# Two sums of w_down's blocks, moved from VectorE in the projection stage to GpSimd in the up stage

## Chip, core and metric

One core of a Trainium2 chip runs the whole kernel. The metric is the device time of one execution in microseconds (us), a median over runs. Engines are named as in the profile: PE is TensorE (PEld its weight loads), DVE is VectorE, ACT is ScalarE, POOL is GpSimd, and SP is the engine that only issues DMAs here, all of them, from one queue and in program order.

## What is computed

A decoder block on 1024 tokens of width 1024: two attention branches mixed by sigmoid gates, then a gated MLP with a causal convolution. The change concerns the end of the mixer and the MLP:

```python
y = jax.nn.sigmoid(g_mla) * (o_mla @ w_o_mla) + jax.nn.sigmoid(g_fox) * (o_fox @ w_o_fox)
...
u = h @ w_up                                   # 1024 x 5632
u = conv_b + sum(conv_w[j] * up[:, j:j + s] for j in range(CONV_WIDTH))
gate, val = u[..., :D_FF], u[..., D_FF:]       # D_FF = 2816
return (jax.nn.silu(gate) * val) @ w_down      # w_down: 2816 x 1024
```

All matrices are float32.

## The kernel before

Each float32 operand is split in a rounded high part (`hi_act`, by ACT, line 82) and the rest (`lo_dve`, line 91, by DVE, or `lo_pool`, line 94, by POOL), and each product is three matmuls, at lines 101 to 103. The MLP's two products run as 2x2 block products with seven instead of eight multiplications, which need sums of blocks of the operands as well. For w_down two such sums are needed, N1 and T2. w_down's rows lie in 22 blocks of 128; for each pair of them (m = 0 to 10), N1 is the left half (columns 0 to 511) of the even block minus its right half, and T2 is the right half of the odd block plus N1. They are made ahead of time, written to DRAM scratch (`dram_N`, `dram_T` in the profile), and read back in the last stage.

**Projection stage** (`mix_and_up`, trace 764 to 862 us). A loop over eight feature blocks d: two products from `w_o_mla` and `w_o_fox` (48 matmuls of 512 columns in all), times the sigmoid gates loaded to tiles `raw` (four buffers in a ring), added, and split into `y`. Two "late rows" are computed in this loop, for g = 5 with d = 1 and for g = 2 with d = 3 (`late_row`): a 512 KB tile is loaded from scratch `dram_acc` into a `raw` buffer, split by ACT and DVE, and summed over partitions by PE (line 311). In the same loop `sum_right` makes N1 and T2 for 11 blocks m of w_down: it loads `dx` (512 KB) and `dz` (256 KB), two buffers each, DVE subtracts (line 973) and adds (line 974), and two stores of 256 KB go out.

**Up stage** (`ffn_up`, trace about 1000 to 1416 us). A loop over 22 columns j of w_up. `operands(j + 1)` loads the next column's two 512 KB tiles `wr` (two buffers) and makes its block sums on DVE (lines 1213 to 1217) and the splits `sh`, `sl`, `vh`, `vl`. PE runs the products of column j; the first four columns have their first and last product for the left half done earlier and have 60 matmuls, later ones 84. DVE reads the banks (lines 1293, 1295), then the convolution (line 1246), a product (line 1306) and, in odd columns, four sums (`stored`, lines 1327 to 1330; on DVE up to j = 7, on POOL later). A second product onto a bank can only start when DVE has read the first one (line 1293, then the product with N4).

**Order.** A scheduler orders the instructions of each engine ahead of time, by its own estimates, with the data dependences kept; so an instruction can stand far from where the code writes it. SP waits at each DMA for what it needs (the data to store, a free buffer, which is the completion of the store that last read it), and all later DMAs wait behind it.

Of the kernel before, what the change touches and what calls it, by code (L numbers as in the profile page):

```python
# [8 lines left out]
F32 = mybir.dt.float32  # L9
# [4 lines left out]
ALU = mybir.AluOpType  # L14
# [58 lines left out]
class Block:  # L73
# [887 lines left out]
    def load_right(self, pool, m):  # L961

        x, z = pool([P, D], F32, "dx", 2), pool([P, 512], F32, "dz", 2)
        self.dma(x, self.a["w_down"][0, 2 * m * P : (2 * m + 1) * P, :])
        self.dma(z, self.a["w_down"][0, (2 * m + 1) * P : (2 * m + 2) * P, 512:1024])
        return m, x, z

    def sum_right(self, pool, d):

        G, V = self.nc.gpsimd.tensor_tensor, self.nc.vector.tensor_tensor  # L970
        lower, upper = HALVES
        for m, x, z in self.blocks:
            V(out=x[:, lower], in0=x[:, lower], in1=x[:, upper], op=ALU.subtract)
            V(out=z, in0=z, in1=x[:, lower], op=ALU.add)
            self.dma(self.place("N1", m), x[:, lower])
            self.dma(self.place("T2", m), z)
        self.blocks = [self.load_right(pool, self.unsummed.pop(0)) for _ in range(2 if 0 < d < 5 else d < 7)]


    def mix_and_up(self):  # L980
# [5 lines left out]
        op, oh, ol = self.op, self.oh, self.ol  # L986
        self.blocks, self.unsummed = [], list(range(NJ // 2))
        for d in range(KD):
# [23 lines left out]
            if d == 4:  # L1012
                self.conv_weights()
            self.sum_right(op, d)
            for late, g in ((1, 5), (3, 2)):
# [232 lines left out]
    def ffn_up(self, tp):  # L1248
# [13 lines left out]
        def first_product(j):  # L1262
            if j < EARLY:
                x = up([P, 512], F32, "p1", 2)
                self.dma(x, self.d_early[j][:, 0, :])
                return x

        def gate(j):
            return (None, None, None) if j < EARLY else self.gate_operands(j)

        ahead, p1 = self.operands(0, gate(0)), first_product(0)
        for j in range(NJ):
            a11, a12, a22, s1, s2, s3, s4 = ahead
# [10 lines left out]
            self.product(x6, s2, "T2", False)  # L1284
            t = copied(x6)
            ug, uv = up([P, S], F32, "u", 6), up([P, S], F32, "u", 6)
            if j < EARLY:
# [19 lines left out]
            if j < NJ - 1:  # L1307
                self.stored(j, act)
        self.last_act = act

# [235 lines left out]
```

## Time and profile before

| | us |
|---|---|
| median of 3 runs (1632.31 to 1634.5) | 1633.96 |
| the profiled execution, its own time | 1631.67 |
| its span, first to last instruction | 1629.9 |
| projection stage, matmuls of d = 0 to 7 | about 764 to 862 |
| residual, second norm and first products of the MLP | about 862 to 1000 |
| up stage | about 1000 to 1416 |
| down stage | about 1416 to 1630 |

A profile's number for an engine is its busy time; PE is the busiest, and its idle time in a stage is time that the stage lost, if nothing else is behind. A row of the timeline gives start, duration, engine, line and tiles, and in brackets how long the engine sat idle before it and what ended that. The granted clock (PEclk) is the share of TensorE's full clock; 0.5 is 1.2 GHz, 1.0 is 2.4 GHz.

### The profile page before, as it was taken

What the parts mean: (1) busy time and instruction counts of PE and PEld (TensorE: products, weight loads), DVE (VectorE), ACT (ScalarE), POOL (GpSimd) and SP (SyncE); (2) the same over time, 40 slices, a digit from 0 to 9 for tenths busy, and PEclk for the clock granted to TensorE, in tenths of its full rate; (3) what the DMA queues carried; (4) which work ended last, traced back from release to release, by engine and by line L of the source; (5) the groups of instructions that cost most, each with busy time, mean ns of one, the idle gap of its engine ahead of it and who ended that gap; (6) DMA issues with size and microseconds to landing.
All of it is one profiled execution on the core that took longest, in us unless ns stands there. A gap on an engine that the chain in (4) does not pass through costs nothing.

```text
span 1629.9 us, 21135 instructions
## 1 busy us (share of the span) xinstructions
PE 1552.7 (95%) x7574; PEld 1274.8 (78%) x7574; DVE 1086.5 (67%) x1741; ACT 776.4 (48%) x1337; POOL 356.8 (22%) x317
## 2 busy tenths in 40 slices
PE   7899989999997999999899978999999999999997
PEld 3778868888886888887687867778888888788886
DVE  5755666566655566575655786988777677746578
ACT  3434345445443555565333444555555455435345
POOL 1322024676671312302020111000011111101010
PEclk9999999999998999999999999999999999999999
DMA  8435487766455434435885425343333332587852
GB/s 286 147 106 162 165 251 198 211 190 184 149 163 134 122 91 128 116 86 203 295 298 194 143 90 168 117 123 97 112 104 111 114 108 99 189 327 288 293 186 104
DMA packets 195191, 271.11 MB, mean 166 GB/s; under 512 B 13090, under 2 KB 114146, under 8 KB 193742
## 3 DMA queue, kind: packets, MB, share of 16 engines
q1 hardware_dynamic: 195086, 269.77, 52.4%
q8 instruction: 59, 0.97, 0.2%
q14 instruction: 46, 0.38, 0.1%
HBM read 187.14 MB, written 70.00 MB: 158 GB/s over the span
## 4 chain that ended last, share of the span: by engine, by line
PE 43%; DVE 4%; DMA 4%; ACT 2%; issue 1%; SPq 0%; ACTq 0%; DVEq 0%
PE ps_mm L101 5%; PE ps_mm L103 5%; PE ps_mm L102 5%; PE ps_sd L101 4%; PE ps_sd L103 4%; PE ps_sd L102 4%; PE ps_x L102 2%; PE ps_x L103 2%; PE ps_x L101 2%; PE ps_y L102 2%; PE ps_y L101 2%; PE ps_y L103 2%; DMA wr_wr<-in_w_up_dram 1%; DVE up_u L1246 1%; DMA o_raw<-dram_acc 1%
## 5 line engine op out<-in xcount | busy, mean ns | idle before, releaser
L101 PE MATMUL psA_fill<-hT_hi,ws_wh 128*128 128x512 f32 x352 | 150.0, 426 | 0.0
L758 ACT ACTIVATE att_p<-psA_s,small_soft 128x128 f32<-128x128 f32 (+7 forms) x128 | 94.8, 740 | 105.4 <-DVE small_soft L752 103.8
L103 PE MATMUL psA_fill<-hT_hi,ws_wl 128*128 128x512 f32 x352 | 139.3, 396 | 0.0
L102 PE MATMUL psA_fill<-hT_lo,ws_wh 128*128 128x512 f32 x352 | 139.3, 396 | 0.0
L94 POOL TENSOR_TENSOR ws_wl<-wr_wr,ws_wh 128x512 fp32r<-128x512 f32 x62 | 83.2, 1346 | 244.6 <-ACT ws_wh L82 221.7
L752 DVE TENSOR_REDUCE small_soft<-psA_s 128x1 f32<-128x128 f32 (+7 forms) x128 | 96.0, 751 | 52.9 <-PE psA_s L750 52.2
L748 PE MATMUL psA_s<-opn_k,opn_q 96*128 96x256 f32 (+7 forms) x480 | 114.6, 359 | 17.3 <-DMA opn_k<-opn_stg 10.9
L1246 DVE SCALAR_TENSOR_TENSOR up_u<-up_u,cw_cw,up_u 128x1023 f32<-128x1023 f32 x88 | 110.7, 1277 | 4.2 <-ACT up_u L1244 4.1
L748 PEld LDWEIGHTS psA_s<-opn_k,opn_q 96*128 96x128 f32 (+1 forms) x480 | 82.1, 192 | 26.7 <-issue 16.6
L760 DVE TENSOR_SCALAR att_p<-att_p,small_soft 128x128 f32<-128x128 f32 (+7 forms) x128 | 86.1, 672 | 4.1
L91 DVE TENSOR_TENSOR att_ptl<-psA_pt,att_pth 128x512 fp32r<-128x512 f32 x96 | 66.0, 687 | 33.3 <-ACT att_pth L82 33.0
L777 PE MATMUL psA_pt<-const_ident,att_p 128*128 128x128 f32 x576 | 86.3, 272 | 0.0
L82 ACT ACTIVATE ring_ah<-ring_ar 128x1024 fp32r<-128x1024 f32 (+1 forms) x41 | 40.4, 985 | 87.5 <-PE ps_x L102 56.9
L91 DVE TENSOR_TENSOR ring_al<-ring_ar,ring_ah 128x1024 fp32r<-128x1024 f32 (+1 forms) x41 | 49.9, 1216 | 45.9 <-ACT ring_ah L82 45.9
L103 PEld LDWEIGHTS psA_fill<-hT_hi,ws_wl 128*128 128x128 f32 x352 | 66.4, 189 | 15.7
L82 ACT ACTIVATE uw_sh<-uw_s 128x1024 fp32r<-128x1024 f32 x44 | 46.7, 1062 | 61.8 <-PE ps_mm L102 29.2
L289 POOL TENSOR_TENSOR att_acc<-att_acc,att_lw 128x512 f32<-128x512 f32 x56 | 74.9, 1337 | 4.2
L101 PEld LDWEIGHTS psA_fill<-hT_hi,ws_wh 128*128 128x128 f32 x352 | 67.4, 191 | 9.6
L102 PEld LDWEIGHTS psA_fill<-hT_lo,ws_wh 128*128 128x128 f32 x352 | 66.9, 190 | 9.7
L91 DVE TENSOR_TENSOR uw_gl<-wr_wr,uw_gh 128x1024 fp32r<-128x1024 f32 x24 | 29.5, 1232 | 65.9 <-ACT uw_gh L82 64.4
L1328 POOL TENSOR_TENSOR up_u<-up_u 128x512 f32<-128x512 f32 x7 | 9.0, 1288 | 263.9 <-DVE up_u L1306 263.9
L82 ACT ACTIVATE att_pth<-psA_pt 128x512 fp32r<-128x512 f32 x96 | 57.2, 595 | 19.8 <-PE psA_pt L777 16.2
(444 smaller groups left out, 4555.6 us busy)
## 6 DMA issues: line engine op xcount, KB each, us to landing
wr_wr<-in_w_up_dram SPq DMA_DIRECT2D x48, 512.0 KB
att_lw<-in_w_ada_dram SPq DMA_DIRECT2D x64, 256.0 KB
wr_wr<-in_w_in_dram SPq DMA_DIRECT2D x28, 512.0 KB
ring_br<-in_w_down_dram SPq DMA_DIRECT2D x24, 512.0 KB
dram_S<-up_u SPq DMA_DIRECT2D x44, 256.0 KB
ring_ar<-dram_S SPq DMA_DIRECT2D x20, 512.0 KB
dram_A<-up_u SPq DMA_DIRECT2D x33, 256.0 KB
ada_wada<-in_w_ada_dram SPq DMA_DIRECT2D x16, 512.0 KB
```

The source lines that it names most:

```text
L82: self.nc.scalar.activation(out, in_, AF.Copy, scale=scale)
L91: self.nc.vector.tensor_tensor(out=out, in0=in_, in1=f32(hi), op=ALU.subtract)
L94: self.nc.gpsimd.tensor_tensor(out=out, in0=in_, in1=f32(hi), op=ALU.subtract)
L101: mm(ps, lhsT=lh, rhs=rh, start=start, stop=False, skip_group_check=onto)
L102: mm(ps, lhsT=lh, rhs=rl, start=False, stop=False, skip_group_check=onto)
L103: mm(ps, lhsT=ll, rhs=rh, start=False, stop=stop, skip_group_check=onto)
L748: mm(o, lhsT=l, rhs=r[:, keys], start=n_ == 0, stop=diag is None and n_ == len(passes) - 1)
L752: nc.vector.tensor_reduce(out=st[:, 0:1], in_=view(s), axis=AX.X if i < 4 else AX.XY, op=ALU.max, negate=True)
L758: nc.scalar.activation(po, view(s), AF.Exp, bias=st[:, 0:1], accum_out=st[:, 1:2])
L760: nc.vector.tensor_scalar(out=pr, in0=pr, scalar1=st[:, 2:3], scalar2=None, op0=ALU.mult)
L777: nc.tensor.transpose(pt[:, n * 256 + e * P : n * 256 + (e + 1) * P], pr[:, kb * P : (kb + 1) * P], self.ident)
L1246: nc.vector.scalar_tensor_tensor(out=dst[:, back:], in0=u[:, : S - back], scalar=cw[:, tap, jj : jj + 1], in1=dst[:, back:], op0=ALU.mult, ...
```

## The change

The sums go from the projection stage to the up stage, from DVE to POOL, and from two buffers of each tile to one:

```diff
     def load_right(self, pool, m):
-        x, z = pool([P, D], F32, "dx", 2), pool([P, 512], F32, "dz", 2)
+        x, z = pool([P, D], F32, "dx"), pool([P, 512], F32, "dz")
         ...
-    def sum_right(self, pool, d):
-        G, V = self.nc.gpsimd.tensor_tensor, self.nc.vector.tensor_tensor
+    def sum_right(self, m, x, z):
+        G = self.nc.gpsimd.tensor_tensor
         lower, upper = HALVES
-        for m, x, z in self.blocks:
-            V(out=x[:, lower], in0=x[:, lower], in1=x[:, upper], op=ALU.subtract)
-            V(out=z, in0=z, in1=x[:, lower], op=ALU.add)
-            self.dma(self.place("N1", m), x[:, lower])
-            self.dma(self.place("T2", m), z)
-        self.blocks = [self.load_right(pool, self.unsummed.pop(0)) for _ in range(2 if 0 < d < 5 else d < 7)]
+        G(out=x[:, lower], in0=x[:, lower], in1=x[:, upper], op=ALU.subtract)
+        G(out=z, in0=z, in1=x[:, lower], op=ALU.add)
+        self.dma(self.place("N1", m), x[:, lower])
+        self.dma(self.place("T2", m), z)
 ...
     def mix_and_up(self):
-        self.blocks, self.unsummed = [], list(range(NJ // 2))
-            self.sum_right(op, d)
 ...
     def ffn_up(self, tp):
-                x = up([P, 512], F32, "p1", 2)
+                x = up([P, 512], F32, "p1", 1)
         ahead, p1 = self.operands(0, gate(0)), first_product(0)
+        block = self.load_right(up, 0)
         for j in range(NJ):
             ...                                  # products N1 and T2 of column j
+            if j % 2 and j < NJ - 1:
+                block = self.load_right(up, (j + 1) // 2)
             ...                                  # the rest of column j
+            if j % 2 == 0:
+                self.sum_right(*block)
```

`p1` holds a finished first product of an early column; it loses a buffer as well.

In the order that results, three places matter. The first is SP's queue in the projection stage, ahead of the load of the second late row (`dram_acc2`). Before (`o_dx`, `o_dz` are the tiles of w_down, `dram_N12` and the like the scratch for the sums):

```order
L79 DMA dram_N12_103_186<-o_dx_26_8087 128x512
L79 DMA dram_T22_109_192<-o_dz_27_8088 128x512
L79 DMA dram_N14_104_187<-o_dx_28_8091 128x512
L79 DMA dram_T24_110_193<-o_dz_29_8092 128x512
L79 DMA o_dx_32_8182<-in_w_down_dram 128x1024
L79 DMA o_dz_33_8183<-in_w_down_dram 128x512
L79 DMA o_dx_34_8186<-in_w_down_dram 128x1024
L79 DMA o_dz_35_8187<-in_w_down_dram 128x512
L79 DMA o_raw_36_8190<-dram_acc2_43_126 128x1024
```

After, at the same load:

```order
L79 DMA o_raw_20_8074<-dram_gate3_20_103 128x1024
L79 DMA o_raw_21_8077<-dram_gate11_28_111 128x1024
L79 DMA wr_wr_57_8234<-in_conv_w_dram 44x3x128
L79 DMA wr_wr_57_8234<-in_conv_b_dram 44x128
L79 DMA wr_wr_58_8244<-in_w_o_mla_dram 128x4x128
L79 DMA o_raw_22_8142<-dram_acc2_43_126 128x1024
```

The four stores and four loads of w_down's blocks are gone from in front of it; gates and weights stand there now.

The second place is SP's queue in the up stage, ahead of the loads of column 3 (`wr_83`, `wr_84`). Before:

```order
L79 DMA up_u_12_9789<-dram_early1_99_182 128x512
L79 DMA wr_wr_83_9852<-in_w_up_dram 128x8x128
L79 DMA dram_A110_56_139<-up_u_7_9723 128x512
L79 DMA wr_wr_84_9854<-in_w_up_dram 128x8x128
```

After, from the loads of column 2 (`wr_81`, `wr_82`) on:

```order
L79 DMA up_dx_14_9709<-in_w_down_dram 128x1024
L79 DMA wr_wr_81_9654<-in_w_up_dram 128x8x128
L79 DMA wr_wr_82_9656<-in_w_up_dram 128x8x128
L79 DMA up_dz_15_9710<-in_w_down_dram 128x512
...
L79 DMA dram_T20_108_191<-up_dz_15_9710 128x512
L79 DMA up_u_16_9713<-dram_early1_99_182 128x512
L79 DMA up_dx_30_9945<-in_w_down_dram 128x1024
L79 DMA up_dz_31_9946<-in_w_down_dram 128x512
L79 DMA dram_N12_103_186<-up_dx_30_9945 128x512
L79 DMA dram_T22_109_192<-up_dz_31_9946 128x512
L79 DMA wr_wr_83_9776<-in_w_up_dram 128x8x128
L79 DMA dram_A110_56_139<-up_u_9_9639 128x512
L79 DMA wr_wr_84_9778<-in_w_up_dram 128x8x128
```

Two whole blocks, with their stores, now stand between the loads of column 2 and those of column 3. In the code block m belongs to column 2m; in this order block 10, the last, is stored before `wr_93`, the first load of column 8.

The third is POOL's order at the start of the up stage. Before, its first work there is a sum of `stored` in a late column:

```order
L94 TENSOR_TENSOR t_N41_10_9338<-gx_x_35_9517,t_N40_9_9337 128x4x128
L1328 TENSOR_TENSOR up_u_69_10911<-up_u_61_10764 128x512
```

After:

```order
L94 TENSOR_TENSOR t_N41_10_9250<-gx_x_35_9429,t_N40_9_9249 128x4x128
L972 TENSOR_TENSOR up_dx_2_9538<-up_dx_2_9538 128x512
L973 TENSOR_TENSOR up_dz_3_9539<-up_dz_3_9539,up_dx_2_9538 128x512
L972 TENSOR_TENSOR up_dx_14_9709<-up_dx_14_9709 128x512
L973 TENSOR_TENSOR up_dz_15_9710<-up_dz_15_9710,up_dx_14_9709 128x512
L972 TENSOR_TENSOR up_dx_30_9945<-up_dx_30_9945 128x512
```

All 22 sums stand there in a row, each bound only by its own loads and stores.

## Rows read from the trace of the kernel before

**Rows 1.** The page: the span and the busiest engine.

```profile
span 1629.9 us, 21135 instructions
PE 1552.7 (95%) x7574; PEld 1274.8 (78%) x7574; DVE 1086.5 (67%) x1741; ACT 776.4 (48%) x1337; POOL 356.8 (22%) x317
```

**Rows 2.** Busy us (and count): PE, PEld, DVE, ACT, POOL; then PEclk, DMA share, GB/s.

```profile
810.00:820.00 10.00, 5.78 (x16) 4.19 (x17) 4.34 (x6) 5.83 (x8) 3.03 (x2) 0.66 0.96 337
```

**Rows 3.** Timeline of PE, projection stage.

```profile
784.25 0.73 PE L311 MATMUL ps_mm<-o_raw,const_ones 128*128 128x512 f32 x2 [1.44 <-ACT o_raw L82]
...
801.28 0.50 PE L101 MATMUL ps_sd<-o_oh,ws_wh 128*128 128x512 f32 x1 [0.50 <-ACT ws_wh L82]
802.64 0.50 PE L103 MATMUL ps_sd<-o_oh,ws_wl 128*128 128x512 f32 x1 [0.39 <-POOL ws_wl L94]
...
814.18 2.48 PE L311 MATMUL ps_mm<-o_raw,const_ones 128*128 128x512 f32 x4 [5.58 <-ACT o_raw L82]
```

**Rows 4.** Timeline of SP's queue, projection stage.

```profile
803.90 0.33 SPq L79 DMA_DIRECT2D o_dx<-in_w_down_dram  x1
...
806.68 0.42 SPq L79 DMA_DIRECT2D o_raw<-dram_acc  x1
```

**Rows 5.** Waits of SP's queue, 740 to 900 us: total, times, longest.

```profile
SPq L79 <- DVE o_dx L973: 12.7, 6, 4.3
SPq L79 <- DMA dram_N<-o_dx: 12.2, 6, 3.3
```

**Rows 6.** The chain that ended last: start, length, what; transfers in three stages.

```profile
759.68 3.18 DMA o_raw<-dram_o
...
806.68 6.38 DMA o_raw<-dram_acc
813.08 1.06 ACT o_raw L82
...
997.50 2.61 DMA up_p<-dram_early
...
1025.77 5.34 DMA wr_wr<-in_w_up_dram
```

**Rows 7.** The sums of before, by line: count, shortest, median, longest ns.

```profile
L973 DVE TENSOR_TENSOR o_dx<-o_dx x11: 676/683/1216, 774.7 to 846.7; 128x512 f32<-128x512 f32 x11
```

**Rows 8.** Busy time by stretch, first columns of the up stage.

```profile
1000.00:1060.00 60.00, 57.13 (x238) 45.89 (x239) 47.57 (x56) 32.79 (x39) 0.00 (x0) 0.95 0.45 134
1060.00:1110.00 50.00, 49.63 (x215) 39.88 (x214) 43.37 (x51) 26.94 (x34) 0.00 (x0) 1.00 0.36 112
```

**Rows 9.** Timeline of SP, DVE, PE and ACT, first columns of the up stage.

```profile
1024.00 0.37 SPq L79 DMA_DIRECT2D wr_wr<-in_w_up_dram  x1
...
1031.21 0.69 DVE L1213 TENSOR_TENSOR uw_s<-wr_wr 128x512 f32<-128x512 f32 x1 [0.68 <-DMA wr_wr<-in_w_up_dram]
...
1043.22 0.50 PE L103 MATMUL ps_mm<-t_N,uw_sl 128*128 128x512 f32 x1 [0.69 <-DVE uw_sl L91]
...
1043.69 0.68 DVE L1293 TENSOR_TENSOR up_u<-ps_sd,up_c 128x512 f32<-128x512 f32 x1
...
1093.74 1.06 ACT L82 ACTIVATE uw_gh<-wr_wr 128x1024 fp32r<-128x1024 f32 x1 [2.22 <-DMA wr_wr<-in_w_up_dram]
```

**Rows 10.** Timeline where POOL and DVE work at once, three places.

```profile
978.06 3.97 POOL L94 TENSOR_TENSOR t_N<-gx_x,t_N 128x512 fp32r<-128x512 f32 x1 [0.74 <-ACT t_N L82]
...
979.66 1.22 DVE L1050 TENSOR_TENSOR gx_h<-gx_h,gx_sf 128x1024 f32<-128x1024 f32 x1
...
1166.61 1.29 POOL L1328 TENSOR_TENSOR up_u<-up_u 128x512 f32<-128x512 f32 x1 [174.35 <-DVE up_u L1306]
...
1415.53 2.21 POOL L1327 TENSOR_TENSOR up_u<-up_u,up_u 128x512 f32<-128x512 f32 x1 [18.92 <-DVE up_u L1306]
1416.51 2.32 DVE L91 TENSOR_TENSOR ring_al<-ring_ar,ring_ah 128x1024 fp32r<-128x1024 f32 x1
```

**Rows 11.** Waits of DVE, 1000 to 1110 us: total, times, longest.

```profile
DVE uw_s L1213 <- DMA wr_wr<-in_w_up_dram: 5.7, 3, 4.3
```

## The prediction

> **What bounds the kernel now.** Read the page first: PE is busy for 95% of 1629.9 us [rows 1], so time moves only where PE stalls. The busy time by stretch finds the stalls: in 810 to 820, where the projection stage ends d = 2 and starts d = 3, PE works 5.78 us of 10 at a mean granted clock of 0.66, while the DMA engines are 96% busy [rows 2]. In the first columns of the up stage PE works 57.13 of 60 and 49.63 of 50 us [rows 8]. PE's timeline then names who is late: twice a late row's tile (line 311) and once the weights of d = 3 [rows 3]. SP's queue and the chain of waits say why: the second late row's load left SP at 806.68, behind a load of w_down at 803.90 [rows 4], and took 6.38 us, where a load of the same 512 KB takes 3.18 elsewhere [rows 6]. In this stage SP waits 12.7 us for the sums and 12.2 for their stores [rows 5], with every later load behind it.
>
> **What the change removes.** PE's idle time at these places is 1.44, then 0.50 + 0.39, then 5.58 us [rows 3]. The clock adds to it: 810 to 820 holds 16 matmuls, and at full clock one takes 49.63 / 215 = 0.231 us [rows 8], so they are worth 3.7 us and the window lost 6.3. The wait began at 814.18 - 5.58 = 808.6 [rows 3], so 1.4 us more lie before the window: 7.7 lost at the second late row, 5.6 by the wait and 2.1 by the clock. Together 1.4 + 0.9 + 7.7 = 10.0. All three have one cause, traffic and stores of w_down ahead in SP's queue, and all of it goes. What is late next there is the `raw` buffer for the second late row, free only some 2.7 us after d = 2's last product (two DVE rows of 1.22 and a hop, an estimate); the load of 3.2 to 5, ACT's split of 1.06 [rows 6] and a DVE row of 1.22 follow: 8 to 10 us, against 48 matmuls of d = 3, or 11.1. It fits with 1 to 3 us to spare; I leave 0 to 1.5 us of loss there. **Gain 8.5 to 10.5, taken as 9.5.** The 22 DVE sums that go (22 x 0.683 = 15 us [rows 7]) are worth nothing more: DVE is busy for 4.34 of 10 us even there [rows 2].
>
> **What it adds: transfers.** Per block 512 + 256 KB loaded and two stores of 256 KB, 14 MB in all, between the w_up loads. DMA is 45% and 36% busy there [rows 8], so bandwidth is at hand; order is what counts. (a) `dx` and `dz` go ahead of the loads of column 1, and `dx` and `p1` ahead of those of column 2: each some 256 to 512 KB more, 1 to 3 us later at 3.18 us for 512 KB [rows 6]. DVE's longest wait for such a load was 4.3 us [rows 11], and PE idled under 3 us in all of these 60 [rows 8], so much of a shift is covered: I take 1, from 0 to 2.5. (b) The loads of column 3 stand behind two blocks. From the landing of `dz_15`, estimated at 1016 because it follows column 2's loads, the queue needs POOL's sum (1.29 [rows 10]), its store (2.0 on average, at most 3.3 [rows 5]), the load of `dz_31` into the same buffer (2.61 [rows 6]), another sum (1.29) and three or four issues at 0.4: 1016 + 1.3 + 2.0 + 2.6 + 1.3 + 1.4 = 1024.6, or 1026 with 3.3 for the store. Before, the first of these loads left at 1024.00 [rows 9]. If POOL waits for DVE as at 978.06 (3.97 in place of 1.29 [rows 10]), the two sums add up to 5.4 more. So 0.6 to 7 us later; I take 3.5, about the middle, as DVE is busy for 47.57 of these 60 us [rows 8]. None of it is covered: DVE waited for these loads already (0.68 us at 1031.21), then worked in one row to 1043, and PE waited 0.69 for its last split at 1043.22 [rows 9].
>
> **What it adds: POOL beside DVE.** POOL has the time: it is idle from the up stage's start to 1166.61, 174 us [rows 10], and 22 x 1.29 = 28.4 us is nothing to it. DVE has not: 47.57 + 43.37 = 90.9 of 110 us [rows 8]. While POOL ran a sum of this shape, DVE's split took 2.32 us at 1416.51, against 1.22 for the same shape at 979.66; in that second case POOL's own row took 3.97 [rows 10]. So one of the two pays, and each sum costs DVE from 0 to 1.1 us. The Trainium skill, "SBUF — State Buffer", section "SBUF: two separate sides", has a rule for this: a DVE instruction with two SBUF inputs and a GpSimd instruction share a port pair as an exclusive lock, and whoever starts first holds it for the whole instruction. By that rule a sum costs DVE up to its full 1.29 us, and 22 of them 28; the row at 1416.51 agrees in kind and shows 1.1. (c) Between the landing of column 3's loads and the read of the bank at 1043.69, DVE's rows stand end to end, and four sums (two blocks) fall there: 0 to 4.4 us, 2 taken, half of it, since POOL loses some of the races. That makes PE's stall at column 3 3.5 + 2 = 5.5 us, and PE has no work ahead to fill it. (d) In columns 3 to 7 the other sums run. DVE's spare time there is 50 - 43.37 = 6.6 us in 50 [rows 8], much of it waiting for PE; twelve sums at 0.55, the middle, are 6.6, and about half should land on idle time: 1 to 5, 3 taken. (e) For a gate tile ACT already waited 2.22 us at 1093.74 [rows 9], and two blocks stand ahead of that load now: 0 to 3, 1 taken. (f) A stall of over 5 us in one piece was followed by matmuls at half clock in 810 to 820, 2.1 us; a like stall at column 3 costs 0 to 2.1, 1 taken.
> **Loss 1 + 5.5 + 3 + 1 + 1 = 11.5, from 3 to 21.** The low end adds 0.6 for (b) and 1 to 2 of the rest; the high end stands at about 2.5 + 7 + 4 + 4 + 2 + 2, as not all ends come together. From column 8 on no sums are left, and the down stage reads N1 and T2 long after the last store: both stay as they are. One buffer of `p1` fewer delays a load that is wanted a column later: nothing.
>
> **The sum.** The profiled execution took 1631.67 us (span 1629.9 and 1.8 around it): 1631.7 - 9.5 + 11.5 = 1633.7. The median of 1633.96 lies 2.3 above that execution, so on its scale **1636**, 0.1% above before. Within 0.2%, 3.3 us, a measurement of this kernel can hardly tell a change: from 1630.7 to 1637.2 is "the same".
>
> **The rivals.** *POOL fits into DVE's gaps.* DVE waits 5.7 us for w_up loads in these 110 us [rows 11], and while a load is late POOL works for free; at 978.06 it was POOL that waited and DVE's row kept its 1.22 [rows 10]. Then (c) and (d) are under 1 together, no stall is long enough for (f), and (a), (b), (e) give 3 to 5: 1634 - 9.5 + 4, about **1628**, faster. Against it: DVE's rows have no gaps where it counts, and in the second place the sum started first. *DVE becomes the bound.* If each sum takes its 1.1 us, columns 2 to 5 lose 4.4 at column 3 and 8 x 0.6 later, with 4 to 5 us of late loads, the clock and (e): 17 to 20 against the 9.5, **1642 to 1645**, slower. It decides as soon as ten sums or so overlap DVE's rows in full, since 10 x 1.1 is more than the spare 6.6 us. *The gain is smaller.* If the second late row is late by its buffer and not by the queue, only 1.4 + 0.9 and some 3 us go, and the loss stays: 1634 - 5 + 11.5, about **1640**. Against it: SP's waits on the sums and their stores add up to 25 us in this stage [rows 5].
>
> A second rule bears on (a) and (b), and only supports them: in "DMA: Bandwidth & Descriptors" of the Trainium skill, section "Queues, rings and completion order", each DMA engine has a ring for each queue, and descriptors of one queue start in order. Were loads of SP's queue free to pass each other, (a) would be nothing; the 6.38 us at 806.68 against 3.18 [rows 6] agree with the rule.
>
> **How the numbers follow.** The forecast, a loss of 8 to 16 and so 1632 to 1641 with 1636 the likeliest, has a chance of 0.47; POOL in the gaps 0.25; DVE as the bound 0.21; the smaller gain 0.07. Of the forecast's 0.47 about 0.32 lie below 1637.2 and 0.15 above; of the first rival 0.22 lie below 1630.7 and 0.03 above. Faster 0.22, the same 0.35, slower 0.15 + 0.21 + 0.07 = 0.43. The range takes in the first rival's middle and the second's: 1627 to 1644.
>
> **What would show it.** Right: no line 311 row with a wait in 764 to 862, granted clock 1.0 in 810 to 820, POOL rows of lines 972 and 973 between about 1000 and 1110, SP waiting for them ahead of column 3's loads, and PE idle for 5 us in two or three pieces around column 3. DVE's splits of 1.22 should read 2.3 beside some of POOL's rows. Wrong: POOL rows of 3 to 4 us with DVE's at 1.22 (first rival), PE stalls in every column to 8 (second), or a wait of line 311 that stays (third). A stall elsewhere, in the norm or the down stage, would be outside all of this.

## The result, and the profile after

| | before | after |
|---|---|---|
| median of 3 runs (us) | 1633.96 | 1650.03 |
| ratio, 95% interval | | 1.0099 [1.0079, 1.0119] |
| projection stage (us) | 101.4 | 90.6 |
| residual, second norm, first products (us) | 134.0 | 135.2 |
| up stage (us) | 418.1 | 445.1 |
| span of the profiled execution (us) | 1629.9 | 1648.2 |

Slower by 1%, 16 us, and outside the stated range. The stages are cut at four rows of PE's timeline that both kernels have: the first product of the projection stage (763.17 before), the weights `wx` (864.54), the first product of column 0 (998.57) and the first stalled row of the down stage (1416.64). So the projection stage gives 10.8 us and the up stage takes 27.1.

The page of the kernel after, first lines, answer to [rows 1]:

```profile
span 1648.2 us, 21133 instructions
PE 1563.8 (95%) x7574; PEld 1284.3 (78%) x7574; DVE 1085.1 (66%) x1719; ACT 776.3 (47%) x1337; POOL 410.0 (25%) x339
```

Busy time by stretch, kernel after (columns as in the first line), answers to [rows 2] and [rows 8]:

```profile
core 0: us, PE busy (x) PEld busy (x) DVE busy (x) ACT busy (x) POOL busy (x), PEclk, DMA share, GB/s
810.00:820.00 10.00, 10.00 (x47) 8.07 (x46) 5.28 (x9) 5.93 (x7) 1.42 (x2) 1.00 0.63 217
1000.00:1060.00 60.00, 51.22 (x211) 40.28 (x210) 46.30 (x48) 28.87 (x34) 23.91 (x9) 0.91 0.65 208
1060.00:1110.00 50.00, 41.59 (x164) 32.88 (x163) 37.14 (x37) 18.29 (x23) 20.98 (x10) 0.90 0.63 200
```

The whole up stage in the same columns, kernel before and kernel after:

```profile
998.57:1416.64 418.07, 413.38 (x1784) 335.82 (x1784) 315.01 (x343) 219.61 (x263) 33.34 (x26) 0.99 0.37 118
989.91:1435.04 445.13, 421.46 (x1784) 340.72 (x1784) 327.66 (x343) 219.01 (x263) 85.57 (x48) 0.97 0.44 143
```

The hole at 810 is full, at clock 1.00. The new hole is in the first columns: PE works 51.22 of 60 and 41.59 of 50 us, where it had 57.13 and 49.63, and the granted clock falls to 0.9. DVE is not busier than before; it waits too. Over the whole stage PE has two losses: it stands idle for longer, and the same 1784 matmuls take 421.46 us in place of 413.38, at a mean granted clock of 0.97 in place of 0.99.

PE's timeline, kernel after, the marks and the longest waits of the up stage:

```profile
764.12 0.50 PE L102 MATMUL ps_mm<-o_ol,ws_wh 128*128 128x512 f32 x1 [0.52 <-DVE o_ol L91]
854.67 1.65 PE L101 MATMUL ps_sd<-wx_w,y_y 128*128 128x512 f32 x3 [2.69 <-ACT wx_w L82]
...
989.91 0.50 PE L101 MATMUL ps_mm<-t_N,uw_sh 128*128 128x512 f32 x1 [2.20 <-ACT uw_sh L82]
...
1034.69 0.80 PE L101 MATMUL ps_mm<-t_B,uw_sh 128*128 128x512 f32 x1 [5.77 <-ACT up_c L1255]
1039.19 0.80 PE L101 MATMUL ps_sd<-t_N,uw_sh 128*128 128x512 f32 x1 [2.42 <-ACT up_c L1255]
...
1078.48 0.80 PE L101 MATMUL ps_sd<-t_N,uw_sh 128*128 128x512 f32 x1 [4.51 <-ACT up_c L1255]
1091.91 0.50 PE L101 MATMUL ps_sd<-t_N,uw_vh 128*128 128x512 f32 x1 [3.90 <-DVE up_u L1292]
...
1113.53 0.58 PE L101 MATMUL ps_sd<-t_N,uw_vh 128*128 128x512 f32 x1 [2.08 <-DVE up_u L1292]
...
1435.04 0.50 PE L102 MATMUL ps_x<-ring_bl,ring_ah 128*128 128x512 f32 x1 [0.76 <-DVE ring_bl L91]
```

No row of line 311 waits any more. In the up stage PE waits 5.77, 2.42 and 4.51 us for ACT's copy of a finished bank (`up_c`) and 3.90 and 2.08 for DVE's read of one. The first two are in column 2, the next two in column 4, the last in column 5. Around the first of them, timelines of SP, POOL, DVE and ACT:

```profile
1010.20 2.35 POOL L973 TENSOR_TENSOR up_dz<-up_dz,up_dx 128x512 f32<-128x512 f32 x1 [1.96 <-issue]
...
1017.21 0.68 DVE L1213 TENSOR_TENSOR uw_s<-uw_s,wr_wr 128x512 f32<-128x512 f32 x1
...
1018.25 2.53 POOL L972 TENSOR_TENSOR up_dx<-up_dx 128x512 f32<-128x512 f32 x1 [5.69 <-DMA up_dz<-in_w_down_dram]
1020.86 2.16 POOL L973 TENSOR_TENSOR up_dz<-up_dz,up_dx 128x512 f32<-128x512 f32 x1
...
1023.04 0.33 SPq L79 DMA_DIRECT2D dram_T<-up_dz  x1
1023.46 1.24 SPq L79 DMA_DIRECT2D wr_wr<-in_w_up_dram  x1
...
1031.77 0.63 ACT L82 ACTIVATE uw_vh<-wr_wr 128x512 fp32r<-128x512 f32 x1 [8.02 <-DMA wr_wr<-in_w_up_dram]
1031.78 0.69 DVE L1209 TENSOR_TENSOR uw_s<-wr_wr 128x512 f32<-128x512 f32 x1 [7.68 <-DMA wr_wr<-in_w_up_dram]
...
1034.06 0.58 ACT L1255 ACTIVATE up_c<-ps_mm 128x512 f32<-128x512 f32 x1
...
1040.88 7.85 POOL L972 TENSOR_TENSOR up_dx<-up_dx 128x512 f32<-128x512 f32 x1 [4.40 <-DMA up_dx<-in_w_down_dram]
...
1047.49 0.68 DVE L1292 TENSOR_TENSOR up_u<-ps_sd,up_c 128x512 f32<-128x512 f32 x1
1048.81 1.30 POOL L973 TENSOR_TENSOR up_dz<-up_dz,up_dx 128x512 f32<-128x512 f32 x1
```

Read it from the top. POOL's two sums of the second block take 2.53 and 2.16 us where one alone takes 1.29 [rows 10]. The store of T2 leaves when the second is done, and 0.4 us behind it the first load of column 3: 1023.46 - 989.91 = 33.55 us after the first product, against 1024.00 - 998.57 = 25.43 before [rows 9], 8.1 us late. DVE and ACT get the tiles 41.9 us after that mark, against 32.6: 9.2 us late. ACT stands 8.02 us at `vh` of column 3, and behind it in ACT's order is the copy of column 2 for which PE waits 5.77. The sum at 1040.88 lasts 7.85 us: ten rows of DVE start in that time, end to end, each at its usual 0.68 or 1.21 us. The sum ends 1.24 us after the start of the ninth of them (1047.49), the first that reads a bank of PE's results (`ps_sd`) and not two tiles in SBUF, the memory in which the tiles lie. So most of the 7.85 us is a wait.

The waits in column 4 are made in the same way. A subtraction of 5.80 us stands in SP's queue ahead of column 5's loads, and ACT and DVE wait for these:

```profile
1057.86 5.80 POOL L972 TENSOR_TENSOR up_dx<-up_dx 128x512 f32<-128x512 f32 x1 [7.76 <-DMA up_dx<-in_w_down_dram]
...
1067.83 1.03 SPq L79 DMA_DIRECT2D wr_wr<-in_w_up_dram  x2
...
1073.21 1.06 ACT L82 ACTIVATE uw_gh<-wr_wr 128x1024 fp32r<-128x1024 f32 x1 [6.10 <-DMA wr_wr<-in_w_up_dram]
...
1074.96 0.69 DVE L1209 TENSOR_TENSOR uw_s<-wr_wr 128x512 f32<-128x512 f32 x1 [7.02 <-DMA wr_wr<-in_w_up_dram]
```

SP's waits in the first columns (990 to 1120 us: total, times, longest) show what it stood for:

```profile
SPq L79 <- POOL up_dx L972: 20.5, 10, 5.9
SPq L79 <- DMA up_dx<-in_w_down_dram: 18.8, 7, 5.5
SPq L79 <- POOL up_dz L973: 17.9, 10, 4.8
```

Who held the first load of column 3 before? Not the queue. SP had stood at it for 10.3 us, and it left 0.02 us after DVE's last block sum of column 2, which frees the tile that the load fills:

```profile
1023.29 0.69 DVE L1217 TENSOR_TENSOR uw_s<-uw_s,wr_wr 128x512 f32<-128x512 f32 x1
```

In the kernel after, the same row of DVE (line 1213, 1017.21 above) ends 28.0 us after the mark, 2.6 later than before. So 2.6 of the 8.1 us would have come from DVE with any queue, and the rest is SP's queue.

### The profile page after: what moved, and what is told of

Same layout as the page of the kernel before. It is cut to its first block, busy times and chain, and to the rows that moved or that the text cites. A ratio compares the mean times of both kernels' runs of the same rounds, so it can differ in the third digit from the quotient of the medians.

```text
span 1648.2 us, 21133 instructions
## 1 busy us (share of the span) xinstructions
PE 1563.8 (95%) x7574; PEld 1284.3 (78%) x7574; DVE 1085.1 (66%) x1719; ACT 776.3 (47%) x1337; POOL 410.0 (25%) x339
## 4 chain that ended last, share of the span: by engine, by line
PE 44%; DVE 4%; DMA 4%; ACT 1%; issue 1%; POOL 1%; SPq 1%; ACTq 0%; POOLq 0%; DVEq 0%
PE ps_mm L101 5%; PE ps_mm L102 5%; PE ps_mm L103 5%; PE ps_sd L101 5%; PE ps_sd L103 5%; PE ps_sd L102 5%; PE ps_x L102 2%; PE ps_x L103 2%; PE ps_x L101 2%; PE ps_y L103 2%; PE ps_y L101 2%; PE ps_y L102 2%; DVE up_u L1242 1%; POOL up_dx L972 1%; DMA wr_wr<-in_w_up_dram 1%
## 5 line engine op out<-in xcount | busy, mean ns | idle before, releaser
L748 PE MATMUL psA_s<-opn_k,opn_q 96*128 96x256 f32 (+7 forms) x480 | 114.9, 359 | 16.0 <-DMA opn_k<-opn_stg 10.1
L1242 DVE SCALAR_TENSOR_TENSOR up_u<-up_u,cw_cw,up_u 128x1023 f32<-128x1023 f32 x88 | 114.9, 1325 | 4.5 <-ACT up_u L1240 4.3
L760 DVE TENSOR_SCALAR att_p<-att_p,small_soft 128x128 f32<-128x128 f32 (+7 forms) x128 | 82.4, 644 | 4.1
L289 POOL TENSOR_TENSOR att_acc<-att_acc,att_lw 128x512 f32<-128x512 f32 x56 | 74.3, 1328 | 4.2
L777 PEld LDWEIGHTS psA_pt<-const_ident,att_p 128*128 128x128 f32 x576 | 66.7, 140 | 0.0
```

Source lines behind the costliest of these rows:

```text
L748: mm(o, lhsT=l, rhs=r[:, keys], start=n_ == 0, stop=diag is None and n_ == len(passes) - 1)
L760: nc.vector.tensor_scalar(out=pr, in0=pr, scalar1=st[:, 2:3], scalar2=None, op0=ALU.mult)
L777: nc.tensor.transpose(pt[:, n * 256 + e * P : n * 256 + (e + 1) * P], pr[:, kb * P : (kb + 1) * P], self.ident)
L1242: nc.vector.scalar_tensor_tensor(out=dst[:, back:], in0=u[:, : S - back], scalar=cw[:, tap, jj : jj + 1], in1=dst[:, back:], op0=ALU.mult, ...
```

## The experiments

All ratios are to runs of the kernel before on the same chip, and the stages come from each run's profile, cut at the rows named above. A stage is read from one execution: the projection stage, the same code in the kernel after and the twelve made from it, takes 90.1 to 91.2 us, so a difference of one microsecond between stages tells nothing. By the medians, which hold the whole time, the runs lie over no_sums by 0.0013 (2 us, within the intervals, dma_only), 0.0065 (11, pool_only), 0.0044 (7, up_dve) and 0.0165 (27, the kernel after).

The question is what makes the up stage 25 to 27 us longer: **queue** (SP's in-order chain of stores and loads ahead of the columns' loads), **bandwidth** (the transfers as such), **port** (POOL's sums and DVE's rows exclude each other), or DVE's own lack of time.

| run | what differs from the kernel after | ratio [95%] | projection | up |
|---|---|---|---|---|
| (before) | | 1 | 101.4 | 418.1 |
| (after) | | 1.0099 [1.0079, 1.0119] | 90.6 | 445.1 |
| no_sums | no sums, loads, stores | 0.9934 [0.9914, 0.9955] | 90.8 | 419.7 |
| dma_only | no sums | 0.9947 [0.9930, 0.9964] | 91.0 | 419.8 |
| pool_only | no loads, stores | 0.9999 [0.9981, 1.0016] | 91.2 | 430.2 |
| own_queue | transfers from POOL's queue | 1.0050 [1.0029, 1.0071] | 90.8 | 435.8 |
| one_sum | 11 sums, not 22 | 1.0042 [1.0022, 1.0061] | 90.7 | 436.3 |
| memsets | two fills for each sum | 0.9968 [0.9952, 0.9985] | 90.8 | 423.0 |
| fill_once | one fill for each sum | 0.9971 [0.9957, 0.9985] | 91.1 | 423.9 |
| up_dve | sums on DVE | 0.9978 [0.9965, 0.9991] | 90.8 | 422.8 |
| act_free | a split from ACT to DVE | 1.0140 [1.0117, 1.0163] | 90.4 | 446.6 |
| spread | a block in each of columns 0 to 10 | 1.0123 [1.0102, 1.0143] | 90.7 | 450.9 |
| late | a block in each of columns 8 to 18 | 0.9966 [0.9951, 0.9980] | 90.1 | 423.7 |
| late_dve | the same, sums on DVE | 1.0032 [1.0020, 1.0045] | 90.5 | 436.3 |
| proj_pool | kernel before, its sums on POOL | 1.0053 [1.0033, 1.0073] | 110.8 | 417.2 |

**What is it worth without the sums?** The run no_sums drops the three lines in `ffn_up`, and the last stage reads blocks of w_down of the same size in place of the sums:

```diff
-        block = self.load_right(up, 0)
 ...
-            if j % 2 and j < NJ - 1:
-                block = self.load_right(up, (j + 1) // 2)
 ...
-            if j % 2 == 0:
-                self.sum_right(*block)
```

> The changed kernel without the two sums, their loads and their stores; the last stage reads blocks of w_down in their place, of the same size, so the output is not the reference's. It shows what the move is worth if the sums were free. In the traces the projection stage lost 10.8 us (763.17 to 864.54 became 764.12 to 854.67) and the up stage gained 27.1 (998.57 to 1416.64 became 989.91 to 1435.04). If the up stage's loss comes from these sums and transfers alone: its length goes back to 418, and the time is 1650 - 27 = 1623, from 1621 to 1626. If the lost second buffer of p1 has a share in it: 1626 to 1635.

The up stage is back at 419.7, 1.6 us over before. Of this 1.2 lie at column 0's second product, where PE waits 3.65 us in place of 2.46 while ACT waits for an `up_p` load; as no block is loaded here, the lost buffer of `p1` is what is left to explain it. The whole gain of the projection stage then shows: 0.9934, some 11 us.

**Transfers or sums?** dma_only drops the sums and keeps all transfers:

```diff
-        G(out=x[:, lower], in0=x[:, lower], in1=x[:, upper], op=ALU.subtract)
-        G(out=z, in0=z, in1=x[:, lower], op=ALU.add)
```

pool_only keeps the sums, on two tiles filled once, and drops the transfers (the last stage reads blocks of w_down, as in no_sums):

```diff
-        self.dma(self.place("N1", m), x[:, lower])
-        self.dma(self.place("T2", m), z)
 ...
-        block = self.load_right(up, 0)
+        block = up([P, D], F32, "dx"), up([P, 512], F32, "dz")
+        nc.gpsimd.memset(block[0], 1.0)
+        nc.gpsimd.memset(block[1], 1.0)
 ...
-            if j % 2 and j < NJ - 1:
-                block = self.load_right(up, (j + 1) // 2)
```

> The changed kernel with all loads and stores of the 11 blocks, in nearly the same order in SP's queue, but without the 22 sums on POOL (the raw blocks are stored, so the output is not the reference's). Theory queue (SP waits in order for a store, then a load, then a sum, and the loads of the columns stand behind): the waits for stores and loads stay, 18.8 + 8.2 + 6.0 us of the 71 that the trace shows, and the waits for the sums, 20.5 + 17.9, go: a loss of 8 to 16 in place of 27, 1631 to 1639. Theory port (POOL's sums stretch DVE's rows): under 4 us of loss, 1623 to 1627. Theory bandwidth (the transfers themselves are too much): the 27 stay, 1646 to 1650.

> The changed kernel with the 22 sums on POOL, on two resident tiles, and no loads and stores for them (the last stage reads blocks of w_down in place of the sums, so the output is not the reference's). POOL can run them as fast as it gets through, at the start of the up stage. Theory queue: SP never waits, the loss is DVE's rows alone, 22 sums of 0.5 us, partly in its gaps: 2 to 6 us, 1625 to 1629. Theory port: each sum costs its full 1.1 us or more on the path and PE's stalls stay: 13 us and more, 1636 to 1650. Theory bandwidth: nothing, 1622 to 1625.

"Queue" as I had it, the waits for stores and loads alone, fails, and so does "bandwidth": 14 MB cost the up stage 0.1 us, and the whole time 2, which is not clear of zero. The sums alone cost 430.2 - 419.7 = 10.5 us, above what "queue" allowed and under "port". Here they run without a break from 979 to 1019, and the timelines of POOL and DVE show both sides paying, row against row:

```profile
1006.48 2.15 POOL L972 TENSOR_TENSOR up_dx<-up_dx 128x512 f32<-128x512 f32 x1
1008.70 2.15 POOL L973 TENSOR_TENSOR up_dz<-up_dz,up_dx 128x512 f32<-128x512 f32 x1
...
1005.17 2.31 DVE L91 TENSOR_TENSOR uw_sl<-uw_s,uw_sh 128x1024 fp32r<-128x1024 f32 x1
1007.40 2.30 DVE L1240 SCALAR_TENSOR_TENSOR up_u<-up_u,cw_cw,up_u 128x1023 f32<-128x1023 f32 x1
1009.63 1.78 DVE L1208 TENSOR_TENSOR uw_s<-wr_wr,wr_wr 128x512 f32<-128x512 f32 x1
```

DVE's 1.22, 1.28 and 0.68 have become 2.31, 2.30 and 1.78. The first load of column 3 leaves 36.4 us after the first product, later than in the kernel after, though SP has no block in its queue: it is held by DVE's late last sum of column 2. But 0.1 + 10.5 is not 25.4 (by the medians 2 + 11 is not 27): the rest appears only with both together.

**SP's chain.** own_queue issues the four transfers of a block from POOL:

```diff
-        self.dma(x, self.a["w_down"][0, 2 * m * P : (2 * m + 1) * P, :])
+        self.nc.gpsimd.dma_start(x, self.a["w_down"][0, 2 * m * P : (2 * m + 1) * P, :])
```

and so for the other three.

> The changed kernel with the four transfers of each block issued by POOL, from its own queue, in place of SP: the same sums, the same bytes, one buffer each, but SP's queue holds only the loads and stores that it held before. Theory queue: the loads of the columns go out when they did before, and the loss falls from 27 to that of the sums beside DVE and of shared bandwidth, 3 to 9: 1626 to 1632. Theory port: 1637 to 1650, as the sums are the same. Theory bandwidth: 1643 to 1650.

The time lies between "queue" and "port", the up stage at 435.8. Taking the chain out of SP's queue gives back 445.1 - 435.8 = 9.3 us; 16.1 of the 25.4 stay without it. The first load of column 3 now leaves at 31.9, again held by DVE's row alone, and two of POOL's subtractions still take 6.73 and 7.43 us.

**Fills in place of sums.** In fill_once (memsets fills each tile twice):

```diff
-        G = self.nc.gpsimd.tensor_tensor
 ...
-        G(out=x[:, lower], in0=x[:, lower], in1=x[:, upper], op=ALU.subtract)
-        G(out=z, in0=z, in1=x[:, lower], op=ALU.add)
+        for y, n in ((x[:, lower], 1), (z, 1)):
+            for _ in range(n):
+                self.nc.gpsimd.memset(y, 1.0)
```

fill_once has the order of the kernel after row for row, in SP's queue and on DVE and ACT; in memsets the scheduler's order differs in places.

> The changed kernel with each sum on POOL replaced by two fills of the same 128x512 tile (POOL MEMSET, 0.53 us each in an earlier run, 22 x 1.06 us in all against 22 x 1.29); loads and stores and SP's waits for POOL stay, and the output is not the reference's. It has POOL's work in SP's chain, but POOL reads no SBUF. Theory port (a POOL sum that reads SBUF and DVE's rows with two SBUF inputs exclude each other): DVE's rows keep their length, POOL's fills too, and the up stage falls from 445.1 to that of the run without sums but with all transfers, 419.8: 420 to 424. Theory chain (any POOL step of about a microsecond between load and store makes the columns' loads late): 432 to 445.

> The changed kernel with each sum on POOL replaced by one fill of the same 128x512 tile (0.53 us); the order in SP's queue is the same row for row, with two whole blocks ahead of column 3's loads (the output is not the reference's). Theory port: POOL's rows stay at 0.53 and DVE's rows are not stretched, and although SP still goes through every store and load in the same order, the up stage is 420 to 423 in place of 445.1. Theory order (two blocks ahead of column 3's loads are too much, whatever POOL does): column 3's loads land 4 us and more later than without blocks, and the up stage is 426 to 438.

423.0 and 423.9: 3.3 to 4.2 us over the run without sums, at the upper end of "port" or just over it. In memsets POOL works 2 x 0.53 us for each sum, not far from the 1.29 of a sum alone, so its time alone is not what costs. The same place in the timelines of fill_once (POOL, SP, DVE):

```profile
1017.28 0.53 POOL L973 MEMSET up_dx<- 128x512 f32 x1 [5.71 <-DMA up_dx<-in_w_down_dram]
1018.09 0.53 POOL L973 MEMSET up_dz<- 128x512 f32 x1 [0.28 <-DMA up_dz<-in_w_down_dram]
...
1019.07 0.40 SPq L79 DMA_DIRECT2D wr_wr<-in_w_up_dram  x1
...
1026.07 0.69 DVE L1209 TENSOR_TENSOR uw_s<-wr_wr 128x512 f32<-128x512 f32 x1 [1.92 <-DMA wr_wr<-in_w_up_dram]
```

Its first column-3 load leaves 1019.07 - 990.91 = 28.2 us after the first product, its DVE row starts at 35.2, not 41.9. All 22 fills keep 0.53 us, and no DVE row from 991 to 1400 is stretched. In the kernel after the 22 sums take 2.37 us in the mean (23.7 us more than at 1.29), and 14 of DVE's rows in the stage are longer than the same rows before, by 12.5 us in all. So of 25.4 us some 4 belong to the order of the queue with a short step on POOL, and 21 to the sums: that they are long, and that DVE's rows and they exclude each other. How these 21 divide between the two the runs do not tell, since a long POOL row is itself the trace of the exclusion.

**Half the sums.** one_sum:

```diff
-        G(out=z, in0=z, in1=x[:, lower], op=ALU.add)
```

> The changed kernel with the first of the two sums of each block only (the output is not the reference's); loads and stores stay, in nearly the same order in SP's queue. Transfers alone cost the up stage 0.1 us, all 22 sums 25.4. If each sum has the same price: 11 of them 12.7, an up stage of 430 to 435. If a late load is a matter of a threshold (as long as the loads of a column come in DVE's slack nothing is lost): under 6, 420 to 426. If the loss is made by the subtraction's long rows (6 to 8 us at two places in the changed kernel): above 435.

436.3: more than half the loss, so no price per sum; it is just over the 435 above which I had put it down to the subtraction's long rows. Four of the 11 subtractions take 4.0 to 5.2 us, as in this row of POOL's timeline, and PE waits 2.24, 2.17, 3.81, 1.27 and 3.04 us in columns 2, 4 and 6.

```profile
1045.43 5.18 POOL L972 TENSOR_TENSOR up_dx<-up_dx 128x512 f32<-128x512 f32 x1 [12.63 <-DMA up_dx<-in_w_down_dram]
```

Half the work on POOL can still meet the wrong moment.

**The sums on DVE, in the up stage.** up_dve:

```diff
-        G = self.nc.gpsimd.tensor_tensor
+        G = self.nc.vector.tensor_tensor
```

> The changed kernel with the 22 sums on DVE in place of POOL, in the up stage. The scheduler spreads them farther: the last block's stores stand ahead of column 12's loads, not of column 8's. No POOL beside DVE, but 22 x 0.68 = 15 us more work on DVE. Theory port with queue (POOL's sums of 1.3 to 7.9 us in SP's chain make the loads late, and stretch DVE): both go, the loss over 419.7 for the up stage without sums is what DVE's 15 us cost beyond its gaps, 2 to 8: 422 to 428. Theory any sum here is too much (DVE is the bound, whoever takes its time): 432 to 445.

422.8, as "port with queue" said: 15 us more work on DVE cost the stage 3.1 (7 by the medians). So DVE had the time; its load alone is not what costs 25 us. The scheduler's order differs here (the blocks reach to column 12), so a part of the difference to 445.1 may be the looser order. This kernel beats the one before, by 0.2%.

**ACT's order.** act_free moves the split at which ACT stood for 8 us:

```diff
-        self.hi_act(vh, v[:, upper])
+        (self.hi_dve if j < 8 else self.hi_act)(vh, v[:, upper])
```

> The changed kernel with one split of a column (vh, high part) made by DVE in place of ACT in columns 0 to 7; the orders of SP and POOL stay as they are. In the changed kernel's trace ACT stands 8.0 us at that split, for the late load of column 3, with the copy of a finished bank behind it, and PE waits 5.77 us for the copy at 1034.69. Theory head of line (ACT's wait in order adds to the loss): that wait of PE goes, and of the up stage's 445.1 us some 4 to 8 go. Theory late load (PE needs the load's own sums soon after anyhow): the stall only moves to column 3's first product, and the up stage stays at 443 to 447, with 0.7 us of DVE added for each column.

The stall only moved. ACT now stands at the silu of column 2 (line 1303), which waits for DVE's convolution, which stands behind DVE's first sum of column 3, which waits for the same load; the copy `up_c` is again behind it (timelines of ACT and PE):

```profile
1034.40 1.06 ACT L1303 ACTIVATE up_u<-up_u 128x1024 f32<-128x1024 f32 x1 [8.53 <-DVE up_u L1242]
1035.36 0.58 ACT L1255 ACTIVATE up_c<-ps_sd 128x512 f32<-128x512 f32 x1
...
1035.99 0.80 PE L101 MATMUL ps_sd<-t_N,uw_sh 128*128 128x512 f32 x1 [7.13 <-ACT up_c L1255]
```

**Other columns.** spread and late tie a block's loads to the product of a column, by a POOL operation on one column of each of the two tiles (here late; spread has `j < 11` and block `j`; late_dve is late with DVE's `G` of up_dve):

```diff
+        if after is not None:
+            for y in (x, z):
+                self.nc.gpsimd.tensor_tensor(out=y[:, 0:1], in0=after[:, 0:1], in1=after[:, 0:1], op=ALU.add)
 ...
+            if 8 <= j < 19:
+                block = self.load_right(up, j - 8, act)
```

> The changed kernel with one block in each of columns 0 to 10: each block's loads wait for that column's last product (a one-element operation of POOL on the tiles ties them), where the changed kernel presses the 11 blocks into columns 0 to 7, two ahead of some columns' loads. Theory chain (two blocks one behind the other, on one buffer each, ahead of the loads of a column is what makes these late): with one block at a time the loss of 25 us falls to that of the sums beside DVE, 22 x 0.5 or so, less its gaps: up stage 424 to 432. Theory per sum (each sum has its price wherever it falls among the first columns): 11 blocks, some in looser columns, 434 to 443.

> The same tie, with one block in each of columns 8 to 18, where PE is busy for the whole time and DVE for 72% of it, and where `stored` already runs on POOL in DVE's gap. If the loss comes from the first columns, where DVE is busy for 83% and the loads of the columns are wanted at once: up stage 418 to 421, and the kernel beats both, 8 to 11 us under the kernel before, like the run without sums. If each sum beside DVE costs its 0.5 to 1.1 us at any place: up stage 430 to 440, slower than before.

> One block in each of columns 8 to 18, as in the run late, with the sums on DVE: no POOL sum stretches a row of DVE (in late 35 rows were stretched, by 32 us, for 4 us of the up stage), and DVE has 0.68 us a sum to do in its idle 28%. Theory port: up stage 419 to 422, 6 to 11 us under the kernel before. Theory DVE's order (a DVE row of a block that waits for its load holds up the column's rows behind it): 424 to 435.

spread (450.9) tells nothing on its question: the tie itself put SP behind the columns' products, as its waits from 985 to 1260 show, and PE still waits 7.39 us at 1219.

```profile
SPq L79 <- DVE up_u L1305: 70.4, 10, 10.5
SPq L79 <- POOL up_dz L966: 19.1, 11, 2.8
```

late loses 4.0 us in place of 25.4, and is faster than both kernels, 0.9966. In these columns DVE was idle for 27% of the time before (busy for 204.48 of 280 us from 1120 to 1400), and though 34 of its rows are stretched, by 32 us, PE hardly waits. That is between my two numbers for it. late_dve (436.3) goes to its rival, just over the 424 to 435: a sum on DVE waits for its load in DVE's order, with the column's rows behind it. DVE's waits, 1120 to 1400 us:

```profile
DVE up_dx L975 <- DMA up_dx<-in_w_down_dram: 19.3, 5, 6.2
```

A sum on POOL may wait there at little cost (4.0 us for all 22); on DVE it may not (16.6).

**The engine alone.** proj_pool is the kernel before with

```diff
-            V(out=x[:, lower], in0=x[:, lower], in1=x[:, upper], op=ALU.subtract)
-            V(out=z, in0=z, in1=x[:, lower], op=ALU.add)
+            G(out=x[:, lower], in0=x[:, lower], in1=x[:, upper], op=ALU.subtract)
+            G(out=z, in0=z, in1=x[:, lower], op=ALU.add)
```

> The kernel before with its 22 sums on POOL in place of DVE, in the projection stage where they were, two buffers each: one part of the change alone. Theory port: DVE is busy for 59 to 72% there and PE's waits are for transfers, so POOL's sums stretch a few rows of DVE and lengthen SP's waits for the sums; the stage from 763.17 to 864.54 (101.4 us) becomes 101 to 106, the time 0 to 5 us over before. If the engine does not matter here and only the place did: 101 to 102, within 0.2% of before. If POOL's longer sums make the late row's load later by their own length: four sums ahead of it at 0.6 to 1.1 us more each, 104 to 107.

9.4 us more in the projection stage, over the largest of the three forecasts. PE's wait of 5.58 us at line 311 shrinks to 0.95 (the other is 1.81, after 1.44), and waits for the projection's weights take its place: 3.93 and 3.47 us for high parts, 1.37 and 1.67 for low parts (`ws_wl`, line 94), which POOL splits behind the sums in its order. SP waits 23.1 us for the sums (740 to 900 us; total, times, longest below), against 12.7 in [rows 5] and 6.0 for line 974 before, but only 8.6 for their stores, against 14.2; then PE's timeline:

```profile
SPq L79 <- POOL o_dz L974: 11.7, 9, 3.1
SPq L79 <- POOL o_dx L973: 11.4, 9, 1.5
...
799.95 0.69 PE L101 MATMUL ps_mm<-o_oh,ws_wh 128*128 128x512 f32 x1 [3.93 <-ACT ws_wh L82]
802.43 0.80 PE L103 MATMUL ps_mm<-o_oh,ws_wl 128*128 128x512 f32 x1 [1.37 <-POOL ws_wl L94]
```

What makes the weights' loads late here (the order that the scheduler chose, or POOL) no run separates. POOL thus costs more than DVE in this stage and in the first columns, and less in columns 8 to 18; that the up stage is the wrong place is not shown, since up_dve and late gain there.

## Why the prediction failed

What PE lost and gained, term by term, from its waits over 0.3 us and its busy time (after less before); waits under 0.3 us make up the 0.2 that is missing to 27.1:

| term of the sum | taken (us) | measured (us) |
|---|---|---|
| gain in the projection stage | 9.5 | 10.8 |
| (a) column 0 | 1 | 1.2, and as much in no_sums |
| (b) + (c), PE's waits in columns 2 and 3 | 5.5 | 7.5 |
| (d) + (e), PE's waits in columns 4 and 5 | 4 | 10.1 |
| (f) granted clock, as PE's busy time | 1 | 8.1 |
| loss in the up stage | 11.5 | 27.1 |

- **The gain: right.** 8.5 to 10.5 was forecast; the stage gave 10.8, and 10.6 in no_sums. All three stalls went, the clock stands at 1.00 from 810 to 820, and the buffer feared as next in line was never late: nothing of the loss stayed. (SP's waits for the sums there were 18.7 us and not 12.7, as line 974 adds 6.0; the gain does not rest on it.)
- **(a): right** that the blocks' first loads cost little. PE waits 3.64 us after 2.46 at column 0's second product, but 3.65 in no_sums as well, so this is not their doing. It falls on `p1`, whose lost buffer was put at nothing.
- **(b): the step that failed.** The first load of column 3 was put 0.6 to 7 us late, 3.5 taken, and came 8.1 late, its data 9.2. The mid value of the chain had put it at 1024.6 - 998.6 = 26.0 after the mark, so 7.5 are missing. 2.9 of these lie in the start (the first block's addition began at 1010.20, where 1016, on a clock now 8.7 earlier, is 1007.3), 1.1 in its length (2.35 for 1.29), and 3.4 in the second block: only one of its sums was counted, though POOL makes the subtraction ahead of the addition, 2.53 + 2.16 = 4.7 where the sum had 1.3. The 3.97 of [rows 10] was kept for the range; the mean of all 22 is 2.37. With one fill in place of each sum the same queue was 28.16 - 25.43 = 2.7 us late, within the range, and half of that is DVE's row, which ends 26.7 us after the mark there. The sum also compared with a departure, 1024.00, that DVE had set and not the queue: it took SP's chain as the only thing that could hold the load. In pool_only and own_queue DVE's stretched rows hold it for 10.9 and 6.4 us longer than before, with no block in SP's queue.
- **(b) was counted once, and this cost more.** The same chain stands ahead of column 5's loads, where a subtraction took 5.80 us. For columns 3 to 7 the sum had only DVE's stretched rows (d) and a wait of ACT (e), 4 us together; PE lost 10.1 there.
- **(c), (d): the kind right, the size low.** 10 of the 14 stretched rows of DVE are longer by 1.0 to 1.1 us, as at 1416.51 in [rows 10], the others by 0.4 to 0.5; 12.5 us in all against 2 + 6.6 before idle time was set off. Twelve sums were counted for columns 3 to 7; in the trace 16 of the 22 start after column 3's loads have left. "DVE wins or POOL wins" was treated as an either-or with a price on one side. The trace shows both at once: POOL's rows are longer by 23.7 us, and these stand in SP's queue ahead of the loads. What the two do together, which no row of the kernel before shows, is what the sum left out: 0.1 for the transfers, 10.5 for the sums, 25.4 together.
- **Who stands behind the late load.** Only DVE's order was followed. ACT's order holds copies of the column before behind the late one's split, and PE waited for those (5.77, 2.42, 4.51). act_free shows that this is not the root: with the split away, DVE's order leads to the same copy.
- **(f): the second step that failed.** One stall was counted, at 0 to 2.1 us. The granted clock is 0.50 in four stretches after 1000, each during or just behind the waits of 2.08 to 5.77 us; before, it was 1.00 from 1010 to 1416. The cost is 421.46 - 413.38 = 8.1 us of PE's busy time, which fits the mean clocks: 413.38 x 0.99 / 0.97 = 421.9. Two of the four, kernel after:

```profile
1032.00:1042.00 10.00, 4.89 (x11) 3.40 (x12) 10.00 (x9) 4.15 (x6) 4.43 (x3) 0.50 0.46 160
1077.00:1083.00 6.00, 4.52 (x11) 3.56 (x12) 6.00 (x5) 1.92 (x3) 1.82 (x2) 0.50 0.60 182
```

- **The rivals.** "DVE becomes the bound", 1642 to 1645, had the right sign and half the reason. pool_only has its mechanism alone, stretched rows of DVE, and loses 10.5; but up_dve gives DVE 15 us more work and loses 3, so DVE's time was not the bound. "POOL fits in the gaps" came near only in columns 8 to 18. The rule of the Trainium skill, "SBUF — State Buffer", section "SBUF: two separate sides", an exclusive lock between a DVE instruction with two SBUF inputs and a GpSimd one that reads SBUF, agrees with the pairs of 2.31 and 2.15 us and with the fills, which read no SBUF and stretched no row of DVE. It was given a price of 28 us and then weighed at half a sum each, on the thought that POOL loses some races for free. It does lose them (7.85 us), but not for free.
- **The signs.** PE's stalls were looked for around column 3 in pieces of 5 us; they are there, and in columns 4 and 5 as well, part of the way to the second rival's sign. No split of 1.22 us reads 2.3 in the kernel after (1.65 to 1.71); the rows that are longer by 1.0 to 1.1 are those of lines 1210, 1242, 1328 and 1329.

## What to carry to other kernels

A sum moved to an idle POOL is not free beside a DVE that is nearly full: price it at what it takes beside DVE's rows, not alone, and then look who waits for its end. If a DMA queue that issues in order stands between, the longer row is paid again in every load behind it; drop the arithmetic but keep the transfers, then the transfers but keep the arithmetic; if the two losses do not add up to the whole, they meet somewhere, and a run with the transfers on another queue tells how much of it the queue makes (here 9.3 of 25.4). Before pricing such a queue, see what held the load until now: a load that waits for its buffer has slack in the queue and none on the engine that frees the buffer. Here it paid to put such work where the full engine has idle time (late: 0.9966), and not where POOL was idle.

## What was not expected of the hardware

- A POOL sum of two SBUF operands, 1.29 us alone, took up to 7.91 us (in act_free) while DVE ran rows end to end, and DVE's rows beside it kept their length. The longest sums of the kernel after (7.85, 5.80 and 2.53 us) end 1.23 to 1.24 us after DVE starts a row that reads a bank of PE's results, and the one of 3.40 ends 1.15 us after DVE falls idle; 6.73 and 7.43 in own_queue and 5.18 in one_sum fit too (1.24 to 1.25). So here a sum that came during such a run of DVE started its work when the run ended. In pool_only the two alternated instead, 2.15 us against a DVE row plus 1.0 to 1.1; why POOL gets its turn there was not found out.
- A fill on POOL (128x512, 0.53 us) is neither stretched nor stretches a row of DVE: 22 of 22 in fill_once.
- Transfers of 14 MB more, at a DMA share of 0.77 to 0.89 between 980 and 1080 us in dma_only, cost the up stage 0.1 us, and 2 us by the medians, not clear of zero.
